# Moving a kernel's operands by 32 bytes: activations, sums and weights at other addresses modulo 256

## The chip, the cores and the metric

The kernel runs on one core of a Trainium2 chip. The metric is the device time of one execution in microseconds (us). A core has five engines that run side by side: TensorE (PE, with its weight loads shown apart as PEld), VectorE (DVE), ScalarE (ACT), GpSimd (POOL) and SyncE (SP), and DMA engines that move data between the large memory (HBM) and the on-chip memory (SBUF). SBUF has 128 partitions; a tile takes the same byte addresses in each of them, and an address below is the byte offset in a partition.

## The reference

One decoder block on an input x of 1 x 256 x 2048 in float32. Cut to what matters:

```
h = rms_norm(x, norm_mix_pre)
p, q, k, v, g, r, gates = split(h @ w_in)            # w_in: 2048 x 11280
y_a = pool_mixer(p) @ w_branch_a                     # 1024 x 2048
o   = rms_norm(gated_linear_attention(q, k, v, g)) * silu(r)
y_b = o @ w_branch_b                                 # 2048 x 2048
mixed = (sigmoid(gates0) * y_a + sigmoid(gates1) * y_b) @ w_out
x = x + rms_norm(mixed)
h = rms_norm(x, norm_ffn_pre)
f = (silu(h @ w_ffn_gate) * (h @ w_ffn_up)) @ w_ffn_down   # 2048 x 5632, 5632 x 2048
out = x + rms_norm(f)
```

Nearly all of the work is products of a 256-row activation with weights that are each used once.

## The kernel before, in words

**Products.** The seven weight matrices are cut into jobs of 512 output columns (one has 528). A job goes through its depth in steps of two blocks of 128 rows (class `Step`). To keep float32 accuracy every operand is split into a high and a low part: ScalarE copies the raw weights into `wh` in the type that TensorE takes at full rate (L340), VectorE subtracts to get `wl` (L344), and each product is made of three matmuls: high x high, high x low, low x high.

- In an ordinary step (L371 to L373) 128x128 of the activation is the stationary operand and 512 columns of `wh` or `wl` are moving.
- In an "across" job (p, q and k; L360 to L362) it is the other way round: a 128x128 piece of the weights is stationary, and 256 columns of the activation are moving.
- 46 jobs do the first 8 blocks of their depth with seven products in place of eight (class `Part`, L431 to L433): sums and differences of blocks of the activation and of the weights are multiplied. The stationary operand is 128x128 of the activation, the moving one 256 columns of weights. Three parts (q1, q2, q4) take plain activation blocks; four (r5, q7, q6, r3) take sums of blocks, prepared by `Act.combine` and held in tiles called x, fx and, for one activation, ox. Weight blocks come in tiles `blocks`; VectorE (L392, L394, L396) and a DMA issued by GpSimd (L403) add them, and L407 and L411 split them.

Each matmul has its own weight load, issued ahead of it, so that the load for the next matmul runs while the present one streams.

**Order.** The program writes the instruction order out: `plan()` lists the jobs, `units` interleaves them, `prepare_to` splits weights some units ahead (four `wh` and four `wl` buffers), and background pieces `bg` and `soon` (activation splits, sums, norms, the recurrent part) are put between units.

**Where things lie.** Tiles come from pools that lie one behind the other in SBUF in the order in which they are opened: `one`, `his` (high parts of activations, and one half of the sums x), `st`, `los` (low parts), `rest` (the other half of x, and Y), `wp` (raw, `wh`, `wl`), `scr`, `blk`, and last `early`, whose place `late` (fx) takes over in the second half. A filler tile `pad` at the head of `his` and of `wp`, which nothing writes or reads, shifts all that follows. `placed` makes a tile with some room and gives back a view of it that starts `lead` bytes into it. `LINE` is 256, and rooms are chosen so that the buffers of a kind agree modulo 256. The layout before and after, as start addresses modulo 256:

| operand | before | after |
|---|---|---|
| activations, high and low (`his`, `los`) | 0 | 32 |
| sums x (`his`, `rest`) and fx (`late`) | 128 | 32 |
| sums ox of o (`early`), qb, kb | 0 | 32 |
| `wh`, `wl` of ordinary steps and across jobs | 64 | 96 |
| `wh`, `wl` of the seven products | 64 | 224 |
| `raw` buffers | 192, 64, 192 | 224, 96, 224 |
| `blocks`, scratch tiles | 64 | 96 |
| x, ident and the other tiles of `one` | 128 | 128 |

Of the kernel before, what the change touches and what calls it, by code (L numbers as in the profile page):

```python
# [8 lines left out]
F32 = mybir.dt.float32  # L9
# [5 lines left out]
P = 128  # L15
# [14 lines left out]
HW = CW // 2  # L30
# [4 lines left out]


LINE = 256
PAD_A, PAD_B, PAD_W = 64, 0, 192
ROOM_W = 4352
AT_X, AT_F = 128, 64  # L40
ROOM_X = 8448
AHEAD = 12
SUMS_AHEAD = 7
# [9 lines left out]
COMBOS = ("r5", "q7", "q6", "r3")  # L53
# [55 lines left out]
def tile_hybrid_block(ctx: ExitStack, tc: tile.TileContext, *aps):  # L109
# [4 lines left out]
    act, dve, pool, pe, sync = nc.scalar, nc.vector, nc.gpsimd, nc.tensor, nc.sync  # L114

    one = ctx.enter_context(tc.tile_pool(name="one", bufs=1))
    his, st, los, rest = [ctx.enter_context(tc.tile_pool(name=n, bufs=b))
                          for n, b in (("his", 1), ("st", 4), ("los", 1), ("rest", 1))]
    wp = ctx.enter_context(tc.tile_pool(name="wp", bufs=BUFS))
# [7 lines left out]
    late = {}  # L127

    def placed(pool, shape, tag, name, lead=0, room=0):

        n = 1
        for k in shape:
            n *= k
        t = pool.tile([P, max(room // 4, n)], F32R, tag=tag, name=name)[:, lead // 4:lead // 4 + n]
        if len(shape) == 2:
            return t.rearrange("p (a b) -> p a b", a=shape[0])
        return t.rearrange("p (a b c) -> p a b c", a=shape[0], b=shape[1])
# [3 lines left out]
    def nm(s):  # L141
        uid[0] += 1
        return f"{s}_{uid[0]}"
# [10 lines left out]
    def f32(ap):  # L154
        return ap.bitcast(F32)


    for p_, n in ((his, PAD_A), (los, PAD_B), (wp, PAD_W)):
        if n:
            p_.tile([P, n // 4], F32, tag="pad", name=nm("pad"), bufs=1)  # L160
    xa = [one.tile([P, D], F32, tag=f"X{t}", name=f"x{t}") for t in range(NT)]
    ident = one.tile([P, P], F32, tag="ident", name="ident")
    masks = two_st.tile([P, 64 * MASKED + P], I32, tag="masks", name="masks")
# [48 lines left out]
    def extra(a):  # L212


        if a.name == "o":
            k = [two_st.tile([P, 2, 4, P], F32R, tag=f"K{i}", name=nm("ox")) for i in range(2)]
            q = [[two_st.tile([P, 4, P], F32R, tag=f"{x}{i}", name=nm("ox")) for i in range(2)] for x in ("Q", "AD")]
            return [tuple(x) for x in q] + [(x[:, 0], x[:, 1]) for x in k]
        if a.name[0] == "f":
            if not late:  # L220
                early.close()
                late["pool"] = ctx.enter_context(tc.tile_pool(name="late", bufs=1, reuse_waits="tile"))
            x = [placed(late["pool"], (len(COMBOS), 4, P), f"fx{i}", nm("fx"), AT_F, ROOM_X) for i in range(2)]
        else:
            x = [placed(pool_, (len(COMBOS), 4, P), f"R{i}", nm("x"), AT_X, ROOM_X) for i, pool_ in enumerate((his, rest))]
        return [(x[0][:, n], x[1][:, n]) for n in range(len(COMBOS))]

    class Act:
# [16 lines left out]
        def combine(self):  # L245

            self.x = {}
            parts = {}
            pieces = extra(self)

            def block(name, g, t):
                parts[name] = scratch().rearrange("p (k c) -> p k c", k=4)
                c = (slice(None), slice(None), slice(t * P, (t + 1) * P))
                dve.tensor_tensor(parts[name], f32(self.hi[g][c]), f32(self.lo[g][c]), op=ALU.add)

            def put(which, name):
                n, src = COMBOS.index(which), parts.pop(name)
                hi, lo = pieces[n]
                act.activation(hi, src, AF.Copy)
                dve.tensor_tensor(lo, src, f32(hi), op=ALU.subtract)  # L260
                self.x[which] = (hi, lo)
                parts[which] = src

            def differ(dst, a, b, op=ALU.subtract):
                dve.tensor_tensor(parts[dst], parts[a], parts[b], op=op)

            return [lambda: (block("21", 0, 1), block("22", 1, 1)),
                    lambda: (differ("22", "21", "22"), put("r5", "22")),
                    lambda: (block("11", 0, 0), differ("21", "11", "21")),
                    lambda: (put("q7", "21"), differ("11", "r5", "11")),  # L270
                    lambda: (put("q6", "11"), block("12", 1, 0)),
                    lambda: (differ("12", "12", "q6", ALU.add), put("r3", "12"))]
# [47 lines left out]
    class Step:  # L320
# [16 lines left out]
        def high(self):  # L337
            self.load()
            self.hi = placed(wp, (GK, self.j.width), "wh", nm("wh"), room=ROOM_W)
            act.activation(self.hi, self.raw, AF.Copy)  # L340

        def low(self):
            self.lo = placed(wp, (GK, self.j.width), "wl", nm("wl"), room=ROOM_W)
            dve.tensor_tensor(self.lo, self.raw, f32(self.hi), op=ALU.subtract)  # L344
# [32 lines left out]
    class Part:  # L377
# [25 lines left out]
                pool.dma_start(self.block((0, 1)), self.block((0, 0)), accum_op=ALU.add)  # L403

        def high(self):
            self.hi = placed(wp, (4, HW), "wh", nm("wh"), room=ROOM_W)
            act.activation(self.hi, self.src, AF.Copy)  # L407

        def low(self):
            self.lo = placed(wp, (4, HW), "wl", nm("wl"), room=ROOM_W)  # L410
            dve.tensor_tensor(self.lo, self.src, f32(self.hi), op=ALU.subtract)  # L411

        def left(self, i):
# [689 lines left out]
```

## Time and profile before

| | |
|---|---|
| median of 3 runs | 1479.87 us (1478.96 to 1480.27) |
| the profiled execution | 1477.55 us, of which its span 1475.7 us |
| instructions | 23511, of which 9156 matmuls |
| DMA | 314.70 MB, mean 213 GB/s |

How to read it: the page gives busy times and a chain of work, followed back from the last instruction to what released each step. Groups of instructions carry a line, an engine, the operation, out<-in by the program's names, the shape, a count, then the busy time in us and the mean duration of one in ns. In a timeline a row is: start in us from the span's start, duration in us, engine, line, operation, names, shape, count. A matmul's duration contains the depth of its pipeline, so that several are under way at once; what one costs in a row of them is the distance between starts. A row of the windows view gives a stretch, its length, the busy time and count of matmuls, the same for weight loads, the granted TensorE clock as a share, the DMA share and GB/s.

### The profile page before, as it was taken

The page shows a single profiled execution, that of the slowest core. Times are in us where ns is not written, and L with a number is a line of the kernel's source. Part 1 is how long each engine was busy: PE and PEld are TensorE (multiplying, and loading weights), DVE is VectorE, ACT ScalarE, POOL GpSimd, SP SyncE. Part 2 cuts the span into 40 slices and gives each one's busy share as a digit, 9 for nine tenths or more (in the row PEclk, how much of TensorE's full clock was granted, in tenths as well). Part 3 has the DMA queues.
Part 4 walks back from the last instruction along what each step waited for, and adds up shares of the span by engine and source line. Part 5 has one row for each costly group of instructions (what it writes and reads, how often), then busy time and mean ns, then how long its engine had stood idle before and what let it go on. Part 6 is the DMA issues. An engine that isn't in the chain of part 4 may idle for free.

```text
span 1475.7 us, 23511 instructions
## 1 busy us (share of the span) xinstructions
PE 1454.2 (99%) x9156; PEld 1299.3 (88%) x9156; DVE 1219.9 (83%) x1359; ACT 907.6 (62%) x1185; POOL 73.0 (5%) x96
## 2 busy tenths in 40 slices
PE   8999999999999999999999999999999999999997
PEld 7988999888888888889878988998998899998886
DVE  6765445789899897799778899888889899889997
ACT  6457433556676665556666666666666666666663
POOL 2000000000110000000000000000000000000001
PEclk9999999999999999999999999999999999999999
DMA  8857765435668688658855677777766777777654
GB/s 286 272 179 230 216 188 182 129 100 184 229 188 258 191 255 259 208 169 283 259 186 158 214 225 220 228 227 230 245 216 212 228 231 228 228 237 229 202 176 144
DMA packets 88896, 314.70 MB, mean 213 GB/s; under 512 B 10140, under 2 KB 10352, under 8 KB 88528
## 3 DMA queue, kind: packets, MB, share of 16 engines
q1 hardware_dynamic: 77616, 279.15, 56.4%
q0 software_dynamic: 8160, 28.59, 10.2%
q10 hardware_dynamic: 3008, 5.45, 1.0%
q8 instruction: 72, 1.18, 0.3%
q14 instruction: 40, 0.33, 0.1%
HBM read 284.84 MB, written 4.19 MB: 196 GB/s over the span
## 4 chain that ended last, share of the span: by engine, by line
PE 85%; DVE 6%; issue 3%; DMA 3%; ACT 2%; POOL 0%; SPq 0%; DVEq 0%; ACTq 0%; POOLq 0%
PE acc L372 15%; PE acc L373 15%; PE acc L371 15%; PE ac L432 5%; PE ac L431 5%; PE ac L433 5%; PE acc L433 4%; PE acc L432 4%; PE acc L431 4%; PE acc L362 3%; PE acc L360 3%; PE acc L361 3%; DVE wl L411 2%; DVE wl L344 2%; PE tr L685 1%
## 5 line engine op out<-in xcount | busy, mean ns | idle before, releaser
L340 ACT ACTIVATE wh<-raw 128x1024 fp32r<-128x1024 f32 (+1 forms) x336 | 355.3, 1059 | 303.3 <-PE acc L373 129.8
L344 DVE TENSOR_TENSOR wl<-raw,wh 128x1024 fp32r<-128x1024 f32 (+1 forms) x336 | 410.5, 1223 | 130.5 <-ACT wh L340 128.0
L411 DVE TENSOR_TENSOR wl<-blocks,wh 128x1024 fp32r<-128x1024 f32 x322 | 390.8, 1222 | 71.6 <-ACT wh L407 69.7
L407 ACT ACTIVATE wh<-blocks 128x1024 fp32r<-128x1024 f32 x322 | 338.5, 1059 | 158.3 <-PE acc L373 65.7
L431 PE MATMUL ac<-wh,x 128*128 128x256 f32 x396 | 110.4, 279 | 0.0
L432 PE MATMUL ac<-wl,x 128*128 128x256 f32 x396 | 109.9, 278 | 0.0
L433 PE MATMUL ac<-wh,x 128*128 128x256 f32 x396 | 109.8, 277 | 0.0
L403 POOL DMA_DIRECT2D blocks<-blocks x46 | 39.9, 867 | 812.9 <-DVE wl L344 209.5
L431 PEld LDWEIGHTS ac<-wh,x 128*128 128x128 f32 x396 | 74.5, 188 | 2.9
L432 PEld LDWEIGHTS ac<-wl,x 128*128 128x128 f32 x396 | 74.4, 188 | 3.1
L433 PEld LDWEIGHTS ac<-wh,x 128*128 128x128 f32 x396 | 74.4, 188 | 0.0
L372 PE MATMUL acc<-wl,h22h 128*128 128x512 f32 x176 | 69.6, 395 | 0.2
L371 PE MATMUL acc<-wh,h22h 128*128 128x512 f32 x176 | 69.4, 394 | 0.2 <-ACT wh L340 0.2
L373 PE MATMUL acc<-wh,h23l 128*128 128x512 f32 x176 | 69.3, 394 | 0.0
L373 PE MATMUL acc<-wh,h22l 128*128 128x512 f32 x176 | 69.2, 394 | 0.0
L372 PE MATMUL acc<-wl,h23h 128*128 128x512 f32 x176 | 69.1, 392 | 0.0
L371 PE MATMUL acc<-wh,h23h 128*128 128x512 f32 x176 | 68.4, 390 | 0.5 <-ACT wh L340 0.5
L396 DVE TENSOR_TENSOR blocks<-blocks,blocks 128x1024 f32<-128x1024 f32 x46 | 56.3, 1223 | 1.3
L392 DVE TENSOR_TENSOR blocks<-blocks,blocks 128x1024 f32<-128x1024 f32 x46 | 56.2, 1221 | 0.7
L394 DVE TENSOR_TENSOR blocks<-blocks 128x1024 f32<-128x1024 f32 x46 | 56.1, 1219 | 0.1
L371 PE MATMUL acc<-wh,h3h 128*128 128x512 f32 (+1 forms) x128 | 49.6, 387 | 0.0
L372 PE MATMUL acc<-wl,h3h 128*128 128x512 f32 (+1 forms) x128 | 49.5, 387 | 0.0
(536 smaller groups left out, 4096.9 us busy)
## 6 DMA issues: line engine op xcount, KB each, us to landing
raw<-in_w_in_dram SPq DMA_DIRECT2D x128, 512.0 KB, 4.1
raw<-in_w_ffn_gate_dram SPq DMA_DIRECT2D x48, 512.0 KB, 4.4
raw<-in_w_ffn_up_dram SPq DMA_DIRECT2D x48, 512.0 KB, 4.4
blocks<-blocks POOLq DMA_DIRECT2D x46, 512.0 KB, 6.1
blocks<-in_w_ffn_down_dram SPq DMA_DIRECT2D x44, 512.0 KB, 4.3
raw<-in_w_ffn_down_dram SPq DMA_DIRECT2D x44, 512.0 KB, 4.4
blocks<-in_w_in_dram SPq DMA_DIRECT2D x40, 512.0 KB, 4.5
blocks<-in_w_ffn_gate_dram SPq DMA_DIRECT2D x40, 512.0 KB, 4.3
```

The costliest lines, as they stand in the source:

```text
L340: act.activation(self.hi, self.raw, AF.Copy)
L344: dve.tensor_tensor(self.lo, self.raw, f32(self.hi), op=ALU.subtract)
L371: pe.matmul(ps, ah, hi[:, i, cs], start=first, stop=False, skip_group_check=j.fast)
L372: pe.matmul(ps, ah, lo[:, i, cs], start=False, stop=False, skip_group_check=j.fast)
L373: pe.matmul(ps, al, hi[:, i, cs], start=False, stop=last, skip_group_check=j.fast)
L392: dve.tensor_tensor(b12, b12, b22, op=ALU.add)
L396: dve.tensor_tensor(b21, b21, b12, op=ALU.add)
L407: act.activation(self.hi, self.src, AF.Copy)
L411: dve.tensor_tensor(self.lo, self.src, f32(self.hi), op=ALU.subtract)
L431: pe.matmul(dst, ah, wh, start=i == 0 and p in ("q1", "r5"), stop=False, skip_group_check=True)
L432: pe.matmul(dst, ah, wl, start=False, stop=False, skip_group_check=True)
L433: pe.matmul(dst, al, wh, start=False, stop=i == 3 and p in EARLY, skip_group_check=True)
```

## The change

The filler ahead of the activations grows from 64 to 96 bytes, and so everything from `his` on lies 32 bytes further. The sums x lose their lead of 128 bytes, the sums fx get 192 in place of 64, and the weights of the seven products get a lead of 128. The filler ahead of `los`, which was 0, goes from the code. No instruction is added, removed or reordered.

```
-PAD_A, PAD_B, PAD_W = 64, 0, 192
+PAD_A, PAD_W = 96, 192
 ROOM_W = 4352
-AT_X, AT_F = 128, 64
+LEAD_FAST = 128
+LEAD_F = 192
 ROOM_X = 8448
...
-    for p_, n in ((his, PAD_A), (los, PAD_B), (wp, PAD_W)):
-        if n:
-            p_.tile([P, n // 4], F32, tag="pad", name=nm("pad"), bufs=1)
+    for p_, n in ((his, PAD_A), (wp, PAD_W)):
+        p_.tile([P, n // 4], F32, tag="pad", name=nm("pad"), bufs=1)
...
-            x = [placed(late["pool"], (len(COMBOS), 4, P), f"fx{i}", nm("fx"), AT_F, ROOM_X) for i in range(2)]
+            x = [placed(late["pool"], (len(COMBOS), 4, P), f"fx{i}", nm("fx"), LEAD_F, ROOM_X) for i in range(2)]
...
-            x = [placed(pool_, (len(COMBOS), 4, P), f"R{i}", nm("x"), AT_X, ROOM_X) for i, pool_ in enumerate((his, rest))]
+            x = [placed(pool_, (len(COMBOS), 4, P), f"R{i}", nm("x"), room=ROOM_X) for i, pool_ in enumerate((his, rest))]
...
         def high(self):
-            self.hi = placed(wp, (4, HW), "wh", nm("wh"), room=ROOM_W)
+            self.hi = placed(wp, (4, HW), "wh", nm("wh"), LEAD_FAST, ROOM_W)
...
         def low(self):
-            self.lo = placed(wp, (4, HW), "wl", nm("wl"), room=ROOM_W)
+            self.lo = placed(wp, (4, HW), "wl", nm("wl"), LEAD_FAST, ROOM_W)
```

## The prediction

> **What bounds the kernel now.** I read the page first: engines, chain, groups. Then the matmuls grouped by shape, then the start times of single matmuls.
>
> ```profile
> span 1475.7 us, 23511 instructions
> PE 1454.2 (99%) x9156; PEld 1299.3 (88%) x9156; DVE 1219.9 (83%) x1359; ACT 907.6 (62%) x1185; POOL 73.0 (5%) x96
> PE 85%; DVE 6%; issue 3%; DMA 3%; ACT 2%; POOL 0%; SPq 0%; DVEq 0%; ACTq 0%; POOLq 0%
> ```
>
> TensorE is busy for 1454.2 of 1475.7 us and holds 85% of the chain that ended last. VectorE has 6% of it, DMA 3%. So an address counts where it alters the time from one matmul to the next; elsewhere it must first get through cover. Three kinds of matmul fill the time. How many there are of each stands in these rows, one per kind, for one of the three lines that issue equally often; the last is the one job with 264-wide matmuls, which belongs to the first kind's lines:
>
> ```profile
> 0.00:1476.00 1476.00, 458.43 (x1184) 222.29 (x1184) 1.00 0.68 213
> 0.00:1476.00 1476.00, 358.93 (x1288) 242.01 (x1288) 1.00 0.68 213
> 0.00:1476.00 1476.00, 107.80 (x384) 71.82 (x384) 1.00 0.68 213
> 63.80:90.30 26.50, 18.43 (x64) 11.93 (x64) 1.00 0.56 178
> ```
>
> They are L371, L431 and L360, and L371 again inside that job. So there are 3 x (1184 - 64) = 3360 ordinary 512-wide matmuls, 3 x 1288 = 3864 of the seven products (256 wide), and 3 x 384 = 1152 "across" ones (256 wide, weights stationary). The granted clock is 1.00 in all four rows: no throttle explains what follows.
>
> What one costs is read from starts, since a duration holds pipeline depth. First and last of four stretches, with the next one's first row as the end:
>
> ```profile
> 113.71 0.39 PE L371 MATMUL acc<-wh,h0h 128*128 128x512 f32 x1
> ...
> 135.68 0.39 PE L371 MATMUL acc<-wh,h0h 128*128 128x512 f32 x1
> ...
> 835.56 0.40 PE L371 MATMUL acc<-wh,h23h 128*128 128x512 f32 x1
> ...
> 838.36 0.28 PE L431 MATMUL acc<-wh,h21h 128*128 128x256 f32 x1
> ...
> 839.78 0.40 PE L371 MATMUL acc<-wh,h22h 128*128 128x512 f32 x1
> ...
> 843.90 0.28 PE L431 MATMUL ac<-wh,h20h 128*128 128x256 f32 x1
> ...
> 845.26 0.28 PE L431 MATMUL acc<-wh,x 128*128 128x256 f32 x1
> ...
> 847.98 0.39 PE L371 MATMUL acc<-wh,h22h 128*128 128x512 f32 x1
> ```
>
> - 113.71 to 135.68: eight steps of 12 matmuls, 21.97 / 96 = 229 ns for a 512-wide one. That is its usual rhythm.
> - 835.56 to 838.36: 2.80 / 12 = 233 ns, the same kind and the same addresses modulo 256 in a slower rhythm.
> - 838.36 to 839.78: 1.42 / 12 = 118 ns, a product in its slow rhythm.
> - 843.90 to 845.26 (distance 64 between the two operands, see below) and 845.26 to 847.98 (distance 192): 1.36 / 12 and 2.72 / 24, both 113.3 ns, the fast rhythm.
>
> Nothing waits inside these stretches. So one pair of addresses allows two rhythms, and two pairs of addresses allow the same one. That is the fact on which I build.
>
> **The change part by part.** Write an operand's place as its start address modulo 256. Before: activations 0, all matmul weights 64, the block sums x and fx 128, the sums ox of o 0. After: activations and all sums 32, ordinary weights 96, product weights 224. What two streams that read at the same time can see of each other is the distance, moving minus stationary:
> ordinary 64 - 0 = 64, after 96 - 32 = 64; across 0 - 64 = 192 modulo 256, after 32 - 96 = 192; products on a sum 64 - 128 = 192, after 224 - 32 = 192; products on plain activations (q1, q2, q4) and on ox 64, after 192.
> No instruction, wait, semaphore, transfer or queue entry is added or removed, and no step is moved past another. So only two things happen: a common shift by 32, and another distance for the plain parts.
>
> *1. Plain parts: distance 64 becomes 192.* Three of seven parts, 3864 x 3/7 = 1656 matmuls, and ox's 96. The present 192 side is read in the same groups:
>
> ```profile
> L432 PE MATMUL ac<-wl,x 128*128 128x256 f32 x396 | 109.9, 278 | 0.0
> L432 PE MATMUL acc<-wl,h21h 128*128 128x256 f32 x160 | 44.2, 277 | 0.0
> L432 PE MATMUL acc<-wl,x 128*128 128x256 f32 x132 | 36.6, 277 | 0.0
> L432 PE MATMUL ac<-wl,fx 128*128 128x256 f32 x132 | 36.9, 280 | 0.7 <-DVE wl L411 0.7
> L432 PE MATMUL ac<-wl,ox 128*128 128x256 f32 x24 | 6.7, 278 | 0.0
> L432 PE MATMUL acc<-wl,f01h 128*128 128x256 f32 x32 | 8.8, 276 | 0.0
> L361 PE MATMUL acc<-h1h,wl 128*128 128x256 f32 x96 | 27.0, 282 | 0.0
> ```
>
> x (192) takes 277 to 278 ns, h21h (64) 277, ox (64) 278: equal in the mean. 276 (f01h) is a group that is nearly all fast, 280 (fx) one that is mostly slow. What differs is how a part enters:
>
> ```profile
> 850.72 0.28 PE L431 MATMUL ac<-wh,x 128*128 128x256 f32 x1
> ...
> 852.10 0.39 PE L371 MATMUL acc<-wh,h23h 128*128 128x512 f32 x1
> ...
> 1116.83 0.28 PE L431 MATMUL ac<-wh,h20h 128*128 128x256 f32 x1
> ...
> 1118.24 0.28 PE L431 MATMUL acc<-wh,x 128*128 128x256 f32 x1
> ...
> 1118.71 0.28 PE L432 MATMUL acc<-wl,x 128*128 128x256 f32 x1
> ...
> 1119.62 0.28 PE L431 MATMUL ac<-wh,x 128*128 128x256 f32 x1
> ```
>
> An x part that follows an ordinary step takes 1.38 us for its 12 instead of 1.36: it pays some 0.01 to 0.02 us. But x also heals: after a stall the plain part h20h runs at 1.41 / 12 = 118 ns, and the x part behind it is back at 0.91 / 8 = 114 ns after four matmuls. If plain parts behave as x does, the cost is at most one entry for two such parts in each of 46 jobs, 92 x 0.015 = +1.4 us, and the gain is the slow plain parts: of 138 about 40 (slow at the share that the means give, 1 ns of the 3 to 4 between 276 and 280), each healed from 1.41 to about 1.38, 40 x 0.035 = -1.4 us. Sum 0. The bounds for all 3864 products: all fast, -0.3 x 3864 x 4.6 ns = -5.3 us; all slow, +0.7 x 3864 x 4.6 = +12.4 us.
>
> *2. Ordinary matmuls: both places 32 further, distance kept.* No row has both at an odd multiple of 32. The nearest is the 264-wide job, whose first half (acc) streams its weights from 64 and 128 and whose second half (tr) from 96 and 160, against activations at 0:
>
> ```profile
> L371 PE MATMUL acc<-wh,h1h 128*128 128x264 f32 x8 | 2.3, 284 | 0.0
> L371 PE MATMUL tr<-wh,h1h 128*128 128x264 f32 x8 | 2.3, 284 | 0.0
> L372 PE MATMUL acc<-wl,h1h 128*128 128x264 f32 x8 | 2.3, 283 | 0.0
> L372 PE MATMUL tr<-wl,h1h 128*128 128x264 f32 x8 | 2.3, 284 | 0.0
> ```
>
> A start at an odd 32 costs 0 to 1 ns there. I take 0: this row is the nearest in kind and the distance stays. The ends are far wider, since the rhythm can flip. High: all at the 233 of 835.56, (233.3 - 229) x 3360 = +14.4 us. Low: the three lines do not take the same time,
>
> ```profile
> L373 PE MATMUL acc<-wh,f03l 128*128 128x512 f32 x32 | 12.6, 394 | 0.0
> L372 PE MATMUL acc<-wl,f03h 128*128 128x512 f32 x32 | 12.5, 392 | 0.0
> L371 PE MATMUL acc<-wh,f03h 128*128 128x512 f32 x32 | 12.4, 388 | 0.0
> ```
>
> and were all like the first line, 391.3 - 388 = 3.3 ns would go: -11.2 us.
>
> A rule that speaks against any effect: the Trainium skill, "TensorE: Matmul & The Clock Gate" (Part 2, step by step), says that TensorE has two independent read ports and that loading the next weights takes no read bandwidth from the running matmul; by its spacing formula a warm 512-wide matmul would follow each 216 ns (an estimate from that page), and no placement could matter: change 0. The trace does not agree, with 229 and 233 ns; so I give the rule no weight.
>
> *3. Across: both 32 further, distance kept.* Mean 282 (row above) is the slow rhythm already. Take 0; low end, all fast, 1152 x 4.6 = -5.3 us, high end 0.
>
> *4. VectorE, ScalarE, DMA.* Their operands move from multiples of 64 to odd multiples of 32. The pooling shifts its operands by 4, 8, 16 and 32 bytes:
>
> ```profile
> L532 DVE TENSOR_TENSOR pt<-pt x4: 682/684/685, 41.1 to 68.7; 128x510 f32<-128x510 f32 x4
> L532 DVE TENSOR_TENSOR qt<-pt x4: 668/682/684, 46.7 to 74.6; 128x508 f32<-128x508 f32 x3, 128x496 f32<-128x496 f32 x1
> L344 DVE TENSOR_TENSOR wl<-raw,wh 128x1024 fp32r<-128x1024 f32 (+1 forms) x336 | 410.5, 1223 | 130.5 <-ACT wh L340 128.0
> ```
>
> 510 elements (shift 4 bytes) take 684 and 1024 take 1223, so 1.05 ns an element; 496 (shift 32) should take 669 and take 668. Cost 0 to 1 ns in 1359 operations, 1.4 us of busy time, of which 6% lies on the chain: 0.1 us. No row has a transfer to an odd 32, nor ScalarE. DMA has 3% of the chain, ScalarE 2%, 74 us together; were both 1% longer or shorter, 0.7 us either way. Take 0. This cover holds only while matmuls are the bound; in the last tenth of the span it is thin.
>
> Sum: 0 + 0 + 0 + 0. The profiled execution took 1477.55 us (span 1475.7 and 1.85 around it), 2.3 below the median of the runs, 1479.87. On that execution I forecast 1477.5, on the median 1479.5, no change.
>
> **The rivals.**
> - *Faster: the common shift counts.* Some boundary that the streams cross, at a multiple of 64 perhaps, is met in a better phase. For it: 3360 ordinary matmuls take 229 ns where two fast 256-wide products take 226.7 with two weight loads, so there is slack; and the same addresses have two rhythms, so phase decides. Against: the 264-wide rows. Price: products all fast alone gives 1479.9 - 5.3 = 1474.6, the ordinary ones alone 1479.9 - 11.2 = 1468.7.
> - *Slower: the same shift puts the ordinary stream into its 233 ns rhythm.* For it: that rhythm stands at 835.56 with present addresses. Against: it is rare. Price 1479.9 + 14.4 = 1494.3; it decides from 3.0 / 3360 = 0.9 ns a matmul on.
> - *The change does not shift anything.* The shift rests on filler tiles that nothing reads or writes; were they dropped, only the leads inside the tiles would act. Nothing in the trace tells it; the time would be 1479.9 within the terms of part 1.
>
> **How the numbers follow.** About 0.2% (3.0 us) is what can be told from no change. No change 0.40 (0.03 of it the third rival), faster by over 0.2% 0.35, slower 0.25. The likeliest is 1479.5, with its own range 1477 to 1483. The range for 8 in 10 takes in most of both ends: 1466 (ordinary ones at their low end and part of the products) to 1492 (most of the +14.4).
>
> **What would show it.** Right: ordinary matmuls still at 229 ns between starts (388, 392, 394 by line), products at 113.3 with fewer at 118 behind a stall, plain and x parts with the same means, VectorE's 1223 ns kept. Wrong: a group of ordinary matmuls whose three means moved together by over 1 ns, or across matmuls that left 282; then the common place counts and not only the distance.

## The result, and the profile after

The kernel after takes 1485.28 us (1484.35 to 1486.04), the kernel before, run beside it, 1479.41 (1475.85 to 1480.27): ratio 1.0046, interval 1.0036 to 1.0056. It is slower by 6 to 7 us: the medians lie 5.9 us apart and the ratio gives 6.8; the spans of the two profiled executions, 1483.2 and 1475.7 us, lie 7.5 apart.

First the page of the kernel after: span, busy times, shares of the chain that ended last.

```profile
span 1483.2 us, 23511 instructions
PE 1466.1 (99%) x9156; PEld 1310.3 (88%) x9156; DVE 1220.5 (82%) x1359; ACT 906.9 (61%) x1185; POOL 72.9 (5%) x96
...
PE 86%; DVE 5%; issue 3%; DMA 3%; ACT 1%; POOL 0%; SPq 0%; DVEq 0%; ACTq 0%; POOLq 0%
...
L344 DVE TENSOR_TENSOR wl<-raw,wh 128x1024 fp32r<-128x1024 f32 (+1 forms) x336 | 410.5, 1223 | 135.2 <-ACT wh L340 134.4
```

VectorE, ScalarE and the chain are what they were (1219.9, 907.6, and 1223 ns for the same operation before). Only TensorE has grown, 1454.2 to 1466.1 us. Some of its groups by shape, kernel after (behind the count and the bar: busy us, mean ns of one):

```profile
L432 PE MATMUL ac<-wl,x 128*128 128x256 f32 x396 | 111.1, 281 | 0.0
...
L432 PE MATMUL acc<-wl,h21h 128*128 128x256 f32 x160 | 44.8, 280 | 0.0
...
L432 PE MATMUL ac<-wl,fx 128*128 128x256 f32 x132 | 37.2, 282 | 0.3 <-DVE wl L411 0.2
...
L361 PE MATMUL acc<-h1h,wl 128*128 128x256 f32 x96 | 27.0, 282 | 0.0
...
L371 PE MATMUL acc<-wh,f03h 128*128 128x512 f32 x32 | 12.6, 395 | 0.0
...
L373 PE MATMUL acc<-wh,f03l 128*128 128x512 f32 x32 | 12.6, 392 | 0.0
...
L372 PE MATMUL acc<-wl,f03h 128*128 128x512 f32 x32 | 12.5, 390 | 0.0
...
L432 PE MATMUL acc<-wl,f01h 128*128 128x256 f32 x32 | 9.0, 280 | 0.0
...
L432 PE MATMUL ac<-wl,ox 128*128 128x256 f32 x24 | 6.7, 280 | 0.0
```

The groups of products shown now have 280 to 282 ns (the same ones before 276 to 280); f01h, nearly all fast before at 276, is at 280. The across group kept its 282. The three ordinary lines of f03 had 388, 392, 394 in the order of issue (L371, L372, L373) and have 395, 390, 392: the same mean within 1 ns, but the short one has moved from the first line to the second. That row, which the prediction quoted for another purpose, turned out to hold the clue.

Durations hold pipeline depth, so I counted starts. A product is "slow" when the next matmul starts 115.5 to 130 ns after it; what is longer counts as a stall. Sums are over all starts of a class, stalls included; means leave out stalls, that is distances over 250 ns (ordinary) or 130 ns (across). Each count comes from the one profiled execution of its kernel:

| | before | after | difference |
|---|---|---|---|
| products on plain activations (1656) | 191.43 us, 526 slow | 195.48 us, 1386 slow | +4.05 us |
| products on x and fx (2112) | 246.59 us, 523 slow | 251.11 us, 1848 slow | +4.52 us |
| products on ox (96) | 11.15 us, 60 slow | 11.24 us, 79 slow | +0.09 us |
| ordinary, 512 wide | 782.1 us, mean 229.46 ns | 781.7 us, mean 229.93 ns | -0.4 us |
| across | 139.7 us, mean 117.16 ns | 139.0 us, mean 117.03 ns | -0.8 us |
| everything from first to last start | 1465.1 us | 1472.6 us | +7.5 us |

The whole loss is products in the 118 ns rhythm: 1109 of 3864 before, 3313 after. They sit where the following answer for one stretch (529 to 537 us, groups of TensorE) shows them, kernel before and then kernel after:

```profile
L431 PE MATMUL acc<-wh,h1h 128*128 128x256 f32 x8 | 2.2, 276 | 0.0
L432 PE MATMUL acc<-wl,h1h 128*128 128x256 f32 x8 | 2.2, 276 | 0.0
L433 PE MATMUL acc<-wh,h1l 128*128 128x256 f32 x8 | 2.2, 276 | 0.0
L373 PE MATMUL acc<-wh,h2l 128*128 128x512 f32 x4 | 1.6, 394 | 0.0
L372 PE MATMUL acc<-wl,h2h 128*128 128x512 f32 x4 | 1.6, 392 | 0.0
L371 PE MATMUL acc<-wh,h2h 128*128 128x512 f32 x4 | 1.6, 388 | 0.0
```

```profile
L433 PE MATMUL acc<-wh,h1l 128*128 128x256 f32 x7 | 2.0, 281 | 0.0
L431 PE MATMUL acc<-wh,h1h 128*128 128x256 f32 x7 | 2.0, 281 | 0.0
L432 PE MATMUL acc<-wl,h1h 128*128 128x256 f32 x7 | 2.0, 281 | 0.0
L371 PE MATMUL acc<-wh,h2h 128*128 128x512 f32 x4 | 1.6, 395 | 0.0
L373 PE MATMUL acc<-wh,h2l 128*128 128x512 f32 x4 | 1.6, 392 | 0.0
L372 PE MATMUL acc<-wl,h2h 128*128 128x512 f32 x4 | 1.6, 390 | 0.0
```

Between starts the ordinary matmuls repeat 226, 229, 232 ns. I call this the beat, and its place the line that has the 226. In this stretch before: 226 at L371, and the products beside it are fast (276). After: 226 at L372, and they are slow (281).

### The profile page after: what moved, and what is told of

It reads as the page before. It is cut to its first block, busy times and chain, and to the rows that moved or that the text cites. A ratio compares the mean times of both kernels' runs of the same rounds, so it can differ in the third digit from the quotient of the medians.

```text
span 1483.2 us, 23511 instructions
## 1 busy us (share of the span) xinstructions
PE 1466.1 (99%) x9156; PEld 1310.3 (88%) x9156; DVE 1220.5 (82%) x1359; ACT 906.9 (61%) x1185; POOL 72.9 (5%) x96
## 3 DMA queue, kind: packets, MB, share of 16 engines
q0 software_dynamic: 8160, 28.59, 10.2%
## 4 chain that ended last, share of the span: by engine, by line
PE 86%; DVE 5%; issue 3%; DMA 3%; ACT 1%; POOL 0%; SPq 0%; DVEq 0%; ACTq 0%; POOLq 0%
PE acc L371 16%; PE acc L373 15%; PE acc L372 15%; PE ac L431 5%; PE ac L432 5%; PE ac L433 5%; PE acc L431 4%; PE acc L433 4%; PE acc L432 4%; PE acc L362 3%; PE acc L360 3%; PE acc L361 3%; DMA raw<-in_w_in_dram 2%; DVE wl L344 2%; PE tr L685 1%
## 5 line engine op out<-in xcount | busy, mean ns | idle before, releaser
L344 DVE TENSOR_TENSOR wl<-raw,wh 128x1024 fp32r<-128x1024 f32 (+1 forms) x336 | 410.5, 1223 | 135.2 <-ACT wh L340 134.4
L371 PE MATMUL acc<-wh,h22h 128*128 128x512 f32 x176 | 70.2, 399 | 0.2 <-ACT wh L340 0.2
L371 PE MATMUL acc<-wh,h23h 128*128 128x512 f32 x176 | 69.4, 395 | 0.0
L373 PE MATMUL acc<-wh,h23l 128*128 128x512 f32 x176 | 69.1, 392 | 0.0
L372 PE MATMUL acc<-wl,h22h 128*128 128x512 f32 x176 | 69.0, 392 | 0.0
L373 PE MATMUL acc<-wh,h22l 128*128 128x512 f32 x176 | 69.0, 393 | 0.0
L372 PE MATMUL acc<-wl,h23h 128*128 128x512 f32 x176 | 68.7, 390 | 0.0
L371 PE MATMUL acc<-wh,h3h 128*128 128x512 f32 (+1 forms) x128 | 49.9, 390 | 0.0
L371 PE MATMUL acc<-wh,h2h 128*128 128x512 f32 (+1 forms) x128 | 49.6, 388 | 0.0
```

The costliest lines, as they stand in the source:

```text
L371: pe.matmul(ps, ah, hi[:, i, cs], start=first, stop=False, skip_group_check=j.fast)
L372: pe.matmul(ps, ah, lo[:, i, cs], start=False, stop=False, skip_group_check=j.fast)
L373: pe.matmul(ps, al, hi[:, i, cs], start=False, stop=last, skip_group_check=j.fast)
```

## The experiments

"Distance" is moving minus stationary start modulo 256, as in the prediction. Ratios are to the kernel before, run beside each group, with 95% intervals. The last three columns are counted from starts, as above, in one execution each; "x" takes in fx. The executions of one kernel can differ: those of sums_only took from 1477.05 to 1485.17 us, and its counts are from one of 1483.71.

| kernel | ratio [interval] | slow products: plain / x / ox | ordinary, ns | across, ns |
|---|---|---|---|---|
| before | 1 | 526 / 523 / 60 | 229.46 | 117.16 |
| after | 1.0046 [1.0036, 1.0056] | 1386 / 1848 / 79 | 229.93 | 117.03 |
| shift_only | 1.0001 [0.9992, 1.0009] | 579 / 614 / 48 | 229.49 | 116.79 |
| dist_only | 1.0053 [1.0041, 1.0065] | 1339 / 1769 / 78 | 229.90 | 117.13 |
| weights_only | 1.0032 [1.0020, 1.0044] | 1240 / 841 / 67 | 229.92 | 117.17 |
| sums_only | 1.0044 [1.0028, 1.0059] | 1555 / 1965 / 96 | 229.25 | 116.94 |
| wl_parts | 1.0064 [1.0047, 1.0081] | 1619 / 1744 / 95 | 229.12 | 116.85 |
| wl_parts_after | 1.0077 [1.0061, 1.0092] | 1506 / 1923 / 94 | 229.95 | 116.98 |
| wl_across | 0.9971 [0.9960, 0.9982] | 667 / 713 / 60 | 229.67 | 113.63 |
| across_dist | 1.0000 [0.9990, 1.0010] | 552 / 566 / 60 | 229.55 | 117.78 |
| wl_across64 | 1.0009 [1.0000, 1.0018] | 586 / 612 / 60 | 229.64 | 118.23 |
| lo_jump | 1.0097 [1.0083, 1.0110] | 1503 / 752 / 95 | 232.36 | 117.78 |
| lo_jump_after | 1.0076 [1.0063, 1.0089] | 775 / 784 / 10 | 233.10 | 117.77 |
| all_jump | 1.0094 [1.0078, 1.0109] | 1572 / 574 / 95 | 232.41 | 117.78 |
| x_lo | 0.9996 [0.9987, 1.0006] | 399 / 836 / 48 | 229.15 | 116.89 |
| x_lo_wl_across | 0.9974 [0.9964, 0.9984] | 432 / 832 / 60 | 229.13 | 113.70 |
| weights_all | 1.0086 [1.0072, 1.0100] | 374 / 1373 / 13 | 233.10 | 117.19 |
| far_lo_jump | 1.0053 [1.0041, 1.0065] | 774 / 774 / 11 | 231.47 | 117.20 |
| split1 | 1.0024 [1.0015, 1.0032] | 1067 / 1392 / 96 | 229.37 | 116.97 |
| split3 | 1.0037 [1.0023, 1.0052] | 1446 / 1870 / 59 | 229.25 | 117.20 |

**1. The change taken apart.** Its pieces are the common shift, the weights of the products, and the places of the sums.

```
shift_only      -PAD_A, PAD_B, PAD_W = 64, 0, 192
                +PAD_A, PAD_B, PAD_W = 96, 0, 192
weights_only    high()/low() of Part: placed(wp, (4, HW), ..., LEAD_FAST=128, ROOM_W)
sums_only       -AT_X, AT_F = 128, 64
                +AT_X, AT_F = 0, 192
dist_only       the edits of weights_only and sums_only together
```

> Only the common shift: the filler ahead of the activations is 96, leads as before, so every operand lies 32 further and every distance is that of before (ordinary 64, plain parts 64, parts on sums 192). Distance theory (only moving minus stationary counts, and the plain parts at 64 held the fast rhythm): as before, 1479 us, about 3 in 10 products slow. Place theory (a product operand at an odd multiple of 32 is slow): 1485 us, over 8 in 10 products at 118 ns between starts. Jump theory (product weights 128 bytes away, modulo 256, from ordinary weights start a part in the slow rhythm): as before, 1479 us.

> Only the distances of the changed kernel, without the shift: activations and all sums at 0, ordinary weights at 64, product weights at 192; all products at distance 192. Distance theory: as the changed kernel, 1485 us, over 8 in 10 products slow. Place theory: 1479 us, as before. Jump theory: 1485 us.

> Before with the product weights alone moved to 192: plain parts at distance 192, parts on sums (at 128) at distance 64, ordinary steps as before. Distance theory: the parts at 64 are now the four on sums and hold the fast rhythm, 1478 to 1481 us, at most 4 in 10 products slow. Jump theory: 1485 us, over 8 in 10 slow, since the product weights lie 128 from the ordinary ones. Place theory: 1479 us.

> Before with the sums alone moved from 128 to 0: all products at distance 64, no part at 192. Distance theory: as before or a little better, 1477 to 1480 us, at most 3 in 10 products slow, and no entry cost of 0.01 us for parts on sums. Jump theory and place theory: as before, 1479 us.

The shift alone does nothing, 1.0001. Distances alone give the whole change, 1.0053. But it is not the distance 192: with the sums alone moved all products lie at distance 64, and it costs 1.0044. The weights alone cost 1.0032, and by groups (their lines are one higher here, wh in 432, wl in 433) only on plain activations; x keeps its 277 to 278 (by starts its class has more slow ones, 841 for 523, but the same sum, 246.6 us):

```profile
L432 PE MATMUL ac<-wh,x 128*128 128x256 f32 x396 | 110.2, 278 | 0.0
L433 PE MATMUL ac<-wl,x 128*128 128x256 f32 x396 | 109.7, 277 | 0.0
L432 PE MATMUL acc<-wh,h21h 128*128 128x256 f32 x160 | 45.5, 284 | 0.0
L433 PE MATMUL acc<-wl,h21h 128*128 128x256 f32 x160 | 44.8, 280 | 0.0
```

So each of the two parts costs most of the loss by itself, and their costs do not add. That took away the theories of places and of distances, and the jump theory as it stood: from the weights alone it expected over 8 in 10 products slow (2148 of 3864 were), from the sums alone no change. The next was that a change of distance heals (junction theory).

**2. Alternating places inside a triple.**

```
wl_parts        before, Part.low(): placed(wp, (4, HW), "wl", ..., 128, room=ROOM_W)
wl_parts_after  after,  Part.low(): placed(wp, (4, HW), "wl", ..., room=ROOM_W)
wl_across       before, Step.low(): placed(..., "wl", ..., 128 if self.j.across else 0, ROOM_W)
across_dist     before, Step.high() and low(): 128 if self.j.across else 0
wl_across64     before, Step.low(): 64 if self.j.across else 0
```

> Edit: in the kernel before, only the low halves of the parts' weights (wl) lie 128 bytes further, at 192; the high halves stay at 64. So the distance (moving minus stationary start, modulo 256) alternates 64, 192, 64 inside every triple of a plain part and 192, 64, 192 inside every triple of a sum part. Junction theory (the two rhythms of the 256-wide products are states that last while the distance stays the same, and a change of distance brings the fast one back): nearly all 3864 products run at 113.3 ns; of the 1109 slow ones of the kernel before some 1000 heal, 1000 x 4.6 ns = -4.6 us, about 1472 us (ratio 0.997). Address-jump theory (only the jump of the stationary operand from a plain block to a sum 128 bytes off heals, at the junction of the parts): the junctions stay as they are, so no change, ratio 1.000. Order theory (only 64 followed by 192 heals, 192 followed by 64 harms): each triple has one of each, no clear change, or slower up to 1.008 if harm wins.

> Edit: in the kernel after, only the low halves of the parts' weights (wl) lie 128 bytes nearer, at 96 instead of 224; high halves stay at 224, activations and all sums at 32. So the distance alternates 192, 64, 192 in every triple of every part, and the stationary addresses do not jump anywhere (all at 32). Junction theory: the slow rhythm does not last, the 3313 slow products of the kernel after fall to a few hundred, -3000 x 4.6 ns = -13.8 us, 1471 to 1473 us (ratio to before 0.995 to 0.998). Address-jump theory: no stationary jump is added, so it stays at 1484 to 1485 us (ratio 1.005).

> Edit: in the kernel before, only the low halves of the weights of the across jobs (wl, there the stationary operand) lie 128 bytes further, at 192. The distance alternates 192, 64, 192 inside their triples. These 1152 matmuls are 256 wide like the products and take 117.2 ns in the mean (slow rhythm 118). Junction theory: they run at 113.3, 1152 x 3.9 ns = -4.5 us, ratio 0.997. Address-jump theory with the stationary operand (here wh at 64, wl at 192 jump by 128 at each load): also heals; so this run tells whether it holds beyond the parts, and the two theories from 'across is slow for another reason', which expects 1.000.

> Edit: in the kernel before, all weights of the across jobs (wh and wl) lie 128 bytes further, at 192. The distance is 64 throughout instead of 192, uniform. Junction theory: a uniform distance does not heal whatever its value, the 1152 matmuls stay at about 117 ns: ratio 1.000 (within 0.001). Distance theory (64 better than 192 in these jobs): fast rhythm, -4.5 us, ratio 0.997.

> Edit: the kernel before with the low halves of the across jobs' weights 64 bytes further, at 128, in place of 128 bytes as in the run that healed these jobs. The stationary start jumps by 64 at each load. If any jump of the stationary start heals: the 1152 across matmuls at about 113.6 ns again, ratio 0.997. If it must be half of 256: they stay at 117 ns, ratio 1.000.

The junction theory fell for products: with the moving operand alternating 3458 and 3523 of 3864 are slow, 1.0064 and 1.0077. In the across jobs, where the same weights are the stationary operand, alternating by 128 healed them, as it expected; a uniform distance or a step of 64 did not. The address-jump theory fell as well, in wl_parts: the stationary start still jumps from a plain block to a sum there, but of 45 sum parts behind a slow plain part none healed. The group of across matmuls with wl, from 282 ns before, in wl_across:

```profile
L361 PE MATMUL acc<-h1h,wl 128*128 128x256 f32 x96 | 26.6, 279 | 0.0
```

The across class fell from 139.7 to 133.8 us, and wl_across is faster than both kernels: 0.9971.

**3. Jumps of the stationary operand in other places.** Low halves of activations or sums 128 bytes away, and all weights 128 further:

```
lo_jump         -PAD_A, PAD_B, PAD_W = 64, 0, 192
                +PAD_A, PAD_B, PAD_W = 64, 128, 64
lo_jump_after   after, with a filler of 128 ahead of los, PAD_W = 64, fx's low half at 160
all_jump        lo_jump, wl_across and fx's low half at 0
x_lo            AT_X * (1 - i) for x, AT_F + 128 * i for fx (high half 128, low half 0)
x_lo_wl_across  both edits
weights_all     lead=128 for every wh and wl
far_lo_jump     lo_jump, lead=128 for every wh and wl, high halves of the sums at 0
```

> Edit: in the kernel before, all low halves of the activations lie 128 bytes further, at 128 (x's low half at 0, its high half at 128; the sums of f and o unchanged), the filler of the weights is 128 bytes smaller so that the weights stay at 64. Now every triple of the ordinary steps, of the plain parts and of the x parts has the stationary operand at 0, 0, 128 (x: 128, 128, 0) and one moving place throughout; in across jobs it is the moving operand that alternates 0, 0, 128 and the stationary that stays. Address-jump theory as it now stands (a jump of the stationary start by 128 from one load to the next brings the fast rhythm; a jump of the moving start takes it away; without a jump the rhythm is carried on): products nearly all fast (1109 slow ones fall to some 150, -4.4 us), ordinary 512-wide ones shorter than 229.5 ns as well if they know the same two rhythms (at least their 371 of 233 ns heal, -1.5 us; at most -11 us), across ones wholly slow (+1 us): 1465 to 1472, ratio 0.992 to 0.997. Across-only theory (what healed the across jobs has to do with their own order of blocks, and jumps of the low halves do nothing for products): ratio 1.000.

> Edit: the kernel after with all low halves of activations and of the sums of x and f 128 bytes further, at 160, and the weights' filler 128 bytes smaller, so that weights stay at 96 and 224. The moving jump between ordinary steps (96) and parts (224) stays, but now every triple holds a jump of the stationary operand. Address-jump theory: each part is thrown into the slow rhythm at its entry and healed within a few matmuls, so the 3313 slow products fall to under 1000: -10 us or more, ratio to before 0.992 to 0.998. If instead the moving place itself (224) makes products slow, they stay slow: ratio 1.005.

> Edit: the kernel before with the low halves of activations at 128 as in the run with that alone, with the low halves of the across jobs' weights at 192, and with the low half of the sums of f at 0. Every class of matmul now has a jump of the stationary operand in each triple; the across jobs have one of the moving operand too. Address-jump theory: the gain of the low halves alone plus that of the across weights (-4.6 us, ratio 0.9971 measured alone): 0.988 to 0.994. If a moving jump inside a triple outweighs the stationary one, across matmuls stay at 117 to 118 ns and only the first gain remains.

> Edit: in the kernel before, only the low halves of the sums x and f's sums are moved, from 128 to 0; their high halves stay at 128, everything else as before. A sum part's triples run at distances 192, 192, 64 by a jump of the stationary start alone; plain and ordinary ones stay uniform at 64, so nothing harms the rhythm there. Majority rule (a triple whose stationary start jumps by 128 is fast if two of its three distances are 192, slow if two are 64; a uniform one carries what it finds): every sum part heals within a few matmuls and passes the fast rhythm on, so the slow products fall from 1109 to 300 to 500: -3 to -4 us, ratio 0.9975. Junction-only theory (the healing needs the change from a plain part to a sum, and jumps inside a triple give nothing more): ratio 1.000.

> Edit: the kernel before with the low halves of the sums at 0 (as in the run with that alone) and the low halves of the across jobs' weights 128 bytes further (as in the run with that alone, ratio 0.9971). Majority rule: both gains add up, across matmuls at 113.6 ns and slow products under 500: ratio 0.994 to 0.996, 1468 to 1471 us. Junction-only theory: only the across gain, 0.997.

> Edit: in the kernel before, all weights of matmuls lie 128 bytes further, at 192 instead of 64, ordinary ones, products' and across jobs' alike; activations at 0 and sums at 128 as before. There is no moving jump anywhere; ordinary and plain run at distance 192 and sums at 64, so the junction from a plain part to a sum goes from 192 to 64 instead of from 64 to 192, by the same jump of the stationary start. Majority rule (only the step to 192 heals): the slow rhythm lasts as with all distances equal, slow products 2500 or more, ratio 1.003 to 1.005. A theory in which any jump of the stationary start by 128 heals at the junction: as before, ratio 1.000.

> Edit: the kernel before with all weights at 192, all low halves of activations and of x's and f's sums at 128, all high halves at 0. Ordinary, plain and sum triples all run at distances 192, 192, 64, by a jump of the stationary start alone; the run with the low halves at 128 and weights at 64 had 64, 64, 192 in ordinary and plain triples and took 1.0097. Across triples have a moving jump (slow, +1 us). Majority rule: products nearly all fast (-4 us or more), ordinary ones back from 232.4 to 229 ns between starts: ratio 0.996 to 0.999. If any jump inside ordinary triples is harmful whatever the order: ordinary ones at 232 ns again, ratio 1.005 or more.

No theory came through all seven. The jump inside a triple did not bring what was expected of it in lo_jump and all_jump (2350 and 2241 slow, ratio 1.0097 and 1.0094). Products did heal where the kernel after had them slow (lo_jump_after: 3313 slow to 1569), but the ordinary matmuls went to 231 to 233 ns, which outweighs it (+9.8 us in that class against -6.2 us in the products, lo_jump_after beside after). far_lo_jump, for which the majority rule wanted 229 ns, has 231.47, nearer to the other expectation (a jump in ordinary triples harms in any order); x_lo, for which it wanted a gain, has none (836 slow on x). There and in x_lo_wl_across the junction-only theory had the time right, 0.9996 and 0.9974. In weights_all both theories missed: it is slower, but by more than the majority rule said and through the ordinary matmuls (+10.2 us) with 1760 slow products in place of 2500 or more. Its groups between 529 and 537 us:

```profile
L431 PE MATMUL acc<-wh,h1h 128*128 128x256 f32 x8 | 2.2, 277 | 0.0
...
L372 PE MATMUL acc<-wl,h2h 128*128 128x512 f32 x4 | 1.6, 396 | 0.0
L373 PE MATMUL acc<-wh,h2l 128*128 128x512 f32 x4 | 1.6, 396 | 0.0
L371 PE MATMUL acc<-wh,h2h 128*128 128x512 f32 x4 | 1.6, 394 | 0.0
```

Ordinary matmuls at 394 to 396 with no short line, plain products fast at 277. No rule that says from distances alone which triple is fast came out of these runs.

**4. The beat.** What did sort the runs in this table, all but the x parts of weights_only, was the place of the 226 in the ordinary step ahead of a part. All parts that directly follow an ordinary step (a part counts by its last six products; "no clear beat": the three lines within 3 ns of each other):

| kernel | 226 at L371 | at L372 or L373 | no clear beat |
|---|---|---|---|
| before | 134 fast, 0 slow | 1 fast, 10 slow | 3 fast, 23 slow |
| sums_only | 13 fast, 0 slow | 0 fast, 155 slow | 1 fast, 2 slow |
| after | 0 fast, 2 slow | 1 fast, 163 slow at L372; 2 slow at L373 | 3 slow |
| weights_only, plain parts | 0 fast, 1 slow | 0 fast, 82 slow | |
| weights_only, x parts | | 81 fast, 1 slow at L372; 5 slow at L373 | 1 slow |

In before, 23 of the 33 slow parts follow a step without a clear beat, on which the table is silent. And where a place changes inside the triple, "226 at L371" does not mean fast: in x_lo, x parts behind such a step are slow in 65 of 65 cases, while plain parts there are fast in 73 of 73. A step and the x part behind it in x_lo, 872.9 to 876.7 us:

```profile
L373 PE MATMUL acc<-wh,h23l 128*128 128x512 f32 x4 | 1.6, 394 | 0.0
L372 PE MATMUL acc<-wl,h23h 128*128 128x512 f32 x4 | 1.6, 392 | 0.0
L371 PE MATMUL acc<-wh,h23h 128*128 128x512 f32 x4 | 1.6, 388 | 0.0
L431 PE MATMUL ac<-wh,x 128*128 128x256 f32 x4 | 1.1, 281 | 0.0
L433 PE MATMUL ac<-wh,x 128*128 128x256 f32 x4 | 1.1, 280 | 0.0
L432 PE MATMUL ac<-wl,x 128*128 128x256 f32 x4 | 1.1, 280 | 0.0
```

The beat outlasts parts and steps alike: in sums_only it stands at the same line on both sides of all but one of the 152 groups of parts that have a clear one on both. The same stretch, 529 to 537 us, in sums_only has it at L373 (388), and slow products:

```profile
L432 PE MATMUL acc<-wl,h1h 128*128 128x256 f32 x7 | 2.0, 279 | 0.0
L372 PE MATMUL acc<-wl,h2h 128*128 128x512 f32 x4 | 1.6, 394 | 0.0
L371 PE MATMUL acc<-wh,h2h 128*128 128x512 f32 x4 | 1.6, 392 | 0.0
L373 PE MATMUL acc<-wh,h2l 128*128 128x512 f32 x4 | 1.6, 388 | 0.0
```

Whether the beat causes the rhythm or only goes with it, two kernels on top of sums_only tell apart: one matmul of a job, or all three of a triple, is issued as two halves, so the count of matmuls moves by one or by three.

```
split1  L371, last ordinary step of each of 46 jobs, first triple:
        -pe.matmul(ps, ah, hi[:, i, cs], ...)
        +[pe.matmul(ps[:, a:b], ah, hi[:, i, a:b], ...) for a, b in ((0, 256), (256, 512))]
split3  the same for L371, L372 and L373 of that triple
```

> Edit: the kernel with the sums alone moved (all products at distance 64, ratio 1.0044), and in the last ordinary step of each of the 46 jobs with seven products one 512-wide matmul (line 371, first of its triple) is issued as two 256-wide ones: one matmul more a job, same work, same places modulo 256. Phase theory (the three-beat of 226, 229, 232 ns goes on by count; a part that follows while the 226 stands at the first line of the triple is fast, else slow): each job shifts the beat by one, so it goes round 1, 3, 2, 1 and about a third of the jobs is fast whatever the stalls do: of 3864 products some 1200 to 1400 fast where that kernel had 248, 1050 x 4.6 ns = -4.8 us against it, ratio to before 1.001 to 1.0025. If the beat belongs to the lines and operands and not to the count: no rotation, 1.004 to 1.005.

> Edit: as the run with one matmul cut, but all three matmuls of that triple are cut in two: three more a job. Phase theory: three more leave the beat where it was, so it stays in the phase that the last stall left, as in the kernel with the sums alone moved: most products slow, ratio 1.003 to 1.006, and no rotation from job to job. If cutting a matmul restores the fast rhythm for another reason (a 256-wide matmul inside an ordinary step, say): as the other run or better, ratio 1.002 or less.

In split1 the beat moved at each of the 46 cuts, and the rhythm went with it: from L372 to L371 21 times, from L371 to L372 17 times, from L373 to L372 7 times, once to L372 from no clear beat. In split3 it stayed at its line at all 46. Groups of the step ahead of a part at 509 to 511 us, then, a job later, the step and part at 529 to 532 us:

```profile
L371 PE MATMUL acc<-wh,h2h 128*128 128x512 f32 x4 | 1.6, 395 | 0.0
L372 PE MATMUL acc<-wl,h2h 128*128 128x512 f32 x4 | 1.6, 390 | 0.0
L373 PE MATMUL acc<-wh,h2l 128*128 128x512 f32 x3 | 1.2, 392 | 0.0
```

```profile
L372 PE MATMUL acc<-wl,h2h 128*128 128x512 f32 x4 | 1.6, 392 | 0.0
L371 PE MATMUL acc<-wh,h2h 128*128 128x512 f32 x4 | 1.6, 388 | 0.0
L373 PE MATMUL acc<-wh,h2l 128*128 128x512 f32 x3 | 1.2, 394 | 0.0
L431 PE MATMUL acc<-wh,h1h 128*128 128x256 f32 x2 | 0.6, 276 | 0.0
L432 PE MATMUL acc<-wl,h1h 128*128 128x256 f32 x2 | 0.6, 276 | 0.0
L433 PE MATMUL acc<-wh,h1l 128*128 128x256 f32 x2 | 0.6, 276 | 0.0
```

Of its 171 parts behind a step, 60 had the 226 at L371 and all were fast; 110 had it at L372 or L373 and all were slow. 1309 products were fast (248 in sums_only), ratio 1.0024 as expected, 3.2 us less span than sums_only (1478.7 against 1481.9). The intervals of split1 and sums_only, up to 1.0032 and from 1.0028, overlap a little, so the counts carry this more than the times. In split3, 22 parts with the 226 at L371 were fast and 105 with it at the other two slow, ratio 1.0037, whose interval includes the 1.0044 of sums_only. So the place of the beat decides where all operands of a kind keep one place and activations and sums share theirs (sums_only and the two cut kernels), and a cut that moves it moves the rhythm. For the change itself, where the moving operand jumps, the same is argued from the table and not from such a cut. That it is a bare count modulo 3 did not hold: the way from L371 should have led to L373 and led to L372.

## Why the prediction was wrong, point by point

- *What bounds the kernel, and where to look.* Right: the loss is in the time between matmul starts, nothing else moved, and the sign came from the two rhythms of one pair of addresses.
- *Part 1, plain parts, distance 64 to 192: "Sum 0".* This is the step that failed. The products cost +8.7 us (4.05 + 4.52 + 0.09), within its ends of -5.3 and +12.4 but near the high one. Four thoughts in it were wrong.
  - "x also heals" was read as a property of the distance 192, to be had for plain parts too. In dist_only plain and sum parts all lie at 192, and of 35 sum parts behind a slow plain part none healed (after: 1 of 37). Before, 9 of 15 do, at the step from plain activations (at 0, distance 64) to sums (at 128, distance 192). Where that step is gone, in sums_only, 0 of 43 do, and the rhythm that a stall leaves lasts until the next stall. The jump from 0 to 128 is not enough by itself: weights_only keeps it, with the distances the other way round, and 0 of 31 heal. What of the step repairs is open.
  - "So only two things happen" left out two more: the change also took away that step between parts, and it made the weights jump from 96 in ordinary steps to 224 in parts. So x and fx, whose distance stays, had no term in the sum, and they cost +4.52 us, over half of the loss.
  - The entry was priced at 0.015 us per part, as if a product would fall back into its rhythm. But with the new jump of the weights the beat is set each time: in the kernel after, every group of parts with a clear beat on both sides, but one of 152, leaves the 226 at L372, also the 6 that were entered with it elsewhere, and behind L372 both kinds are slow there. In weights_only the same holds for those entered with it elsewhere (8 of 8); plain parts behind a step are slow there, while x parts, with another place than plain ones, are fast (81 of 82 behind L372).
  - The 280 of fx was read as "mostly slow"; by starts 123 of its 528 products were. The share of slow plain parts that was drawn from it, 40 of 138, is near the 526 of 1656 that were counted, by luck.
- *Part 2, ordinary matmuls, 0.* Right in the sum, -0.4 us, and shift_only's 1.0001 shows it for the shift by itself. Its "low end" (all like the first line) misread the row: 388, 392, 394 are not three prices but a beat whose place moves, and in no run did all three lines have the short one (the lowest class mean is 229.12 ns).
- *Part 3, across, 0.* Right, 117.16 to 117.03 ns. The "all fast" end of -5.3 us was real: wl_across took 5.9 us from this class.
- *Part 4, VectorE, ScalarE, DMA, 0.* Right: 1223 ns again, DMA 3% of the chain again.
- *The rule weighed.* From the two independent read ports of the Trainium skill, "TensorE: Matmul & The Clock Gate" (Part 2, step by step), the prediction worked out that placement could not matter, and it rightly gave this no weight: kernels that differ in start places alone went from 0.9971 to 1.0097.
- *Rivals.* None came true. The slower one named the ordinary stream at 233 ns; that stayed away here, though weights_all (233.10) shows that a move of 128 brings it. A slower rival for products, all in their slow rhythm at up to +12.4 us, stood only as a bound and should have been one with a chance of its own. "Slower" had 0.25, for the other reason. That 1485.28 lies between 1466 and 1492 is luck: those ends were set by the ordinary matmuls, whose sum moved by 0.4 us.
- *What would show it.* "Products at 113.3 with fewer at 118" was wrong. "Plain and x parts with the same means" came, but with both slow. The sign set for a common shift, three ordinary means moving together, did not come: they changed places.

What stays open: why a part entered with the 226 at L371 is fast, and which jumps set the beat where. The table in part 4 says what happened in these kernels; it predicts no others. That the change loses by both causes is shown only so far as each alone gives most of the loss.

## What to carry to other kernels

Where one engine runs without gaps, a cheap step can have two stable rhythms, and its mean says how often it is in which. Before pricing a change that makes places alike, count in the trace what throws the step from one rhythm into the other and what brings it back: here the change removed the one step between parts at which it was repaired. Read the lines of one loop body separately too, since a fixed order of their mean durations can be a beat whose place tells what the next part will do.

## What was unexpected of the hardware

- Ordinary 512-wide matmuls at one pair of places repeat 226, 229, 232 ns between starts, keep that phase through dozens of steps and products, and cutting one of them in two moves it.
- Where operands keep one place, that phase decides whether the 256-wide products that follow take 113.3 or 118 ns: of 171 parts in split1, 60 of 60 were fast behind one phase and 110 of 110 slow behind the others. Products in the slow rhythm cost the change 8.7 us of 1480.
- A stationary operand that alternates by 128 bytes took across matmuls from 117.16 to 113.63 ns; by 64 bytes it did not (118.23); the moving operand alternating by 128 left products slow.
- All weights 128 bytes further put 512-wide matmuls from 229.46 to 233.10 ns, while 32 bytes for all operands alike changed nothing (229.49 ns, ratio 1.0001).
